# Weights of a mixture of experts loaded two chunks at a time, in 1 MB transfers of 8 KB per partition

## The chip, the cores and the metric

The kernel runs on one core of one Trainium2 chip. The metric is the device time of one execution in microseconds (us); lower is better.

## The reference

One layer over 2048 tokens of 1024 channels in fp32: a mixer (a long convolution over half of the channels, a Fourier transform over the other half, head norms and an output projection), then a mixture of 32 experts of which each token takes two, then a last norm. What matters here is the experts' part:

```python
def expert_block(args):
    e, rows_tok, rows_w = args
    xb = tok[rows_tok]                      # 128 tokens x 1024
    a = xb @ w_gate[e]                      # 1024 x 512
    u = xb @ w_up[e]                        # 1024 x 512
    y = (jax.nn.silu(a) * u) @ w_down[e]    # 512 x 1024
    return (y * rows_w[:, None].astype(y.dtype)).astype(tok.dtype)
...
out = jnp.zeros((T, D), tok.dtype).at[row_tok].add(ys.reshape(n_rows, D))
```

The three weight matrices of an expert have 2 MB each, 192 MB in all.

## The kernel before

The mixer fills the first half of the time. Routing then sorts the 32 experts by their counts into turns; `eid` holds the expert of each turn, and `gia`, `gib`, `sia`, `sib` hold the rows to gather and to add to. Each expert has 128 slots. The experts of the first 18 ranks (`RANK[e] < NOV`) have 32 more slots, the overflow tokens, whose rows are gathered as four quarters on four groups of 32 partitions (`xo`).

**Chunks.** `seq` lists 384 chunks of weights of 512 KB: four for each of gate, up and down of each expert, in the order of use. `load(n)` (L862) allocates a raw tile of 128 x 1024 fp32 and starts its transfer, on SP's queue for nearly all chunks and on POOL's for the eight of the first experts' down matrices. A gate or up chunk is 256 rows of 512 columns, row block k on columns 512 k of the tile (L880); a down chunk is 128 rows of 1024 columns (L883). The raw tiles rotate through three rings: 16 buffers (`NRAW`, tag `wr`), 4 (`NEXT`) and 4 (`NMORE`). The first 16 chunks are loaded while the mixer's last tiles are at work (L1357), the others by `take` (L1401), which hands out the next chunk for use and calls `load` up to 28 chunks ahead. A load waits on its queue until its buffer is free.

**Cuts.** `cut(n)` (L1387) splits a raw chunk into two parts in fp32r: ACT rounds it to `h` (L1391) and DVE takes the rest `l` (L1392; POOL for every second chunk of the last 24). Cuts run two chunks ahead of their use.

**Products.** `turn(e)` (L1525) transposes the 128 gathered rows `xg` with eight products against the identity on PE (L1533) and splits them into `xh` and `xl`; `turn_o(e)` (L1539) transposes the overflow rows `xo` with two (L1546). `gate_up` (L1550) makes six products of 512 columns for each chunk (L1563). `over` (L1575) multiplies the overflow tokens with the raw chunks in fp32, each product on one of four groups of 32 columns of the array (L1583); it runs once for the four chunks of a matrix, so these buffers come free together. `turn_s` (L1600) transposes the inner activations `s` (L1607) and, for overflow tokens, `so` with two products over 64 partitions (L1615). `down` (L1619) multiplies with the down chunks (L1631, L1637), scales the result on ACT (`yt`) and adds it to the rows of `X2` in DRAM with accumulating scatters issued by POOL (L1650, L1652). `between` (L1654) puts `turn_s(e)` and `turn(e + 1)` into the middle of the product before, and gathers three experts ahead.

**The end.** `bulk` (L1429) reads the 16 tiles of `X2` back into the ring of `wr` buffers (L1437), squares them on ACT (L1427), scales them on DVE (L1453) and stores the output (L1454), while the last two experts are still at work; those get their norm in `finish` (L1475).

Instructions of one engine run in the order of the program as it was scheduled when built; a waiting instruction holds up those behind it on its engine or queue. The tiles' semaphores make a load wait for all readers of the buffer that it overwrites.

Of the kernel before, what the change touches and what calls it, by code (L numbers as in the profile page):

```python
# [9 lines left out]
F32 = mybir.dt.float32  # L10
# [9 lines left out]
P = 128  # L20
# [25 lines left out]
# experts are taken by their counts: the first ones get 32 slots beyond the 128  # L46
NFIX = 2
# the first experts' 128 slots take tokens of the first tiles only
# [13 lines left out]
def _ranks():  # L62
    """The rank by count of the expert at each turn."""
    n, few = NE - NFIX - NLAST, NE - NOV - NLAST
    many, rest = iter(range(NFIX, NOV)), iter(range(NOV, NE))
    mid = [next(rest) if (i + 1) * few // n > i * few // n else next(many) for i in range(n)]
    return list(range(NFIX)) + mid + list(rest)
# [18 lines left out]
def fft_tables(T):  # L86
    """A transform of 4096 points in two stages: n = 64 a + p, p = 16 m + g, k = r + 64 k2.

    The first one sums over a and turns by exp(-2 pi i r n / 4096), r = 0..31 (r = 0 stands for 0 and 32, both
    real before the turn); the second one sums over p.  # L90
    """
# [11 lines left out]
    w = first(64 * a[None, :, None] + 16 * m[None, None, :] + g[:, None, None])     # [g, a, m, comp]  # L103
    wu = np.zeros((16, 2, 2, 32, 2, 2, 2, 64))      # [g, m % 2, part of z, a, m // 2, pass, m % 2, comp]
# [9 lines left out]
    w = first(32 * np.arange(P)[None, :] + np.arange(32)[:, None]).reshape(32, 64, 2, 64)     # [q, a, x, comp]  # L114
# [25 lines left out]
    # the inverse leaves p in the order 4 g + m  # L140
# [5 lines left out]
def tables():  # L146
# [16 lines left out]
    # real and imaginary parts of a 64-point transform, two groups at once  # L163
# [6 lines left out]
    # transform over t, folded twice: t < 512, bins k = 2 k' + parity  # L170
# [14 lines left out]
    # routing: tokens, counted from one, in the order of their tiles; rows of ranks  # L185
# [6 lines left out]
    # order of the experts: their numbers as tie breakers, ranks of the turns, masks  # L192
# [14 lines left out]
def build(tc, I, out, dbg=None, upto=99):  # L207
# [4 lines left out]
    with es:  # L212
# [8 lines left out]
        # Fourier columns of tiles 0..3 and 8..11; those of tiles 15 - k and 7 - k, with the row that follows, are read backwards  # L221
# [16 lines left out]
        def rsq(dst, src, scale, pool, n, tag, ln=False):  # L238
            """dst = (src * scale + EPS) ** -0.5"""
# [9 lines left out]
            # one Newton step for what the tables leave  # L249
# [8 lines left out]
        # ------------------------------------------------------------------ mixer, first part  # L258
# [15 lines left out]
        with ExitStack() as e1, ExitStack() as e2:  # L274
# [31 lines left out]
            def cutg(hi, lo, w):  # L306
                """hi and lo of w times the first norm's gain, a number for every row."""
# [19 lines left out]
            def conv(c, wvec, sink):  # L327
                """Projection chunk c through the short filter, a quarter of t for every call; sink(q, piece)."""
# [33 lines left out]
            def to_rows(src, dst):  # L362
                """[channel, 512 t] to [t, channel] rows of DRAM, in one or two parts, after the next products."""
# [16 lines left out]
            def sinks(c):  # L380
                """Filter and use of chunk c: v (8..11) is kept for x1 (4..7), whose product with it is z."""
# [13 lines left out]
            with tc.tile_pool(name="pa", bufs=1) as pa:  # L395
                # per-channel vectors: short filter (3 x 12), its bias (12), gains of heads and of the first norm
# [57 lines left out]
            def wprime(g):  # L454
                """Fourier columns of the projection, with the transform along a head folded in."""
# [28 lines left out]
            def ktaps(q):  # L484
                """The filter's taps 32 i + q, and the absolute sum so far."""
# [30 lines left out]
            def ksum(kt):  # L516
                """The kernel's absolute sum; the skip weight goes in as a tap at lag 0."""
# [32 lines left out]
            # implicit filters' features: partitions = (half of t, feature)  # L550
# [46 lines left out]
            def spread():  # L597
                """Features of t on the lower half of the partitions, of 2048 - t on the upper one."""
# [44 lines left out]
            def fweights(h):  # L643
                """Weights of half h of the Fourier columns, in two parts."""
# [8 lines left out]
            def fourier(h, i, wh, wl, pm, dst=None):  # L653
                """Fourier columns of tile i, rows = t, to DRAM or to where they are used."""
# [68 lines left out]
            def prod(o, w, xh, xl):  # L723
                """o = w x, both in two parts."""
                for n, (a, b) in enumerate(((0, xh), (0, xl), (1, xh))):
                    T.matmul(o, w(a), b, start=n == 0, stop=n == 2)

            def residue(n):
# [6 lines left out]
                if n == 0:  # L735
                    # the real bins 0 and 32 and those between them
# [8 lines left out]
                else:  # L745
                    # real parts on the lower half of the partitions, imaginary ones on the upper half
# [35 lines left out]
            def begin(t):  # L782
                """Rows t and 1024 + t of the fold, the first half of the columns where the second one comes straight."""
# [9 lines left out]
            def pair(t):  # L793
                """Sums and differences of rows t and L - t, and of 1024 + t and 1024 - t."""
                rr = rrs.pop(t)
                pq = []
                for k in range(2):
                    # groups of 66 real parts and 62 imaginary ones
# [9 lines left out]
            # Fourier columns, rows = t  # L808
# [41 lines left out]
        # ------------------------------------------------------------------ Fourier mixing, output projection  # L850
# [11 lines left out]
        def load(n):  # L862
            e, m, c = seq[n]
            k = n % (NRAW + NEXT + NMORE)
            if k < NRAW:
                w = mw.tile([P, 1024], F32, tag="wr", bufs=NRAW, name="w")
            elif k < NRAW + NEXT:
                w = ring[0].tile([P, 1024], F32, tag="wx", bufs=NEXT, name="w")
            else:
                w = ring[1].tile([P, 1024], F32, tag="wx", bufs=NMORE, name="w")  # L870
# [8 lines left out]
            if m < 2:  # L879
                q.dma_start(w.rearrange("p (k f) -> p k f", k=2),  # L880
                            src[:, 256 * c:256 * c + 256, :].rearrange("a (k p) f -> p (a k) f", p=P))
            else:
                q.dma_start(w, src[:, P * c:P * c + P, :].rearrange("a p f -> p (a f)"))  # L883
            raws[n] = w
# [3 lines left out]
        def gather(e, part=(0, 1)):  # L888
# [4 lines left out]
            if 1 in part and RANK[e] < NOV:  # L893
                xo_[e] = mw.tile([P, 256], F32, tag="xo", bufs=2, name="xo")
                x = G.indirect_dma_start(xo_[e], None, XR.rearrange("t (q c) -> (t q) c", q=4),
                                     bass.IndirectOffsetOnAxis(ap=gb[:, e:e + 1], axis=0))
                if e < NFIX:
                    # the queue goes on with these cuts while the rows are unknown
# [3 lines left out]
        # the first gathers come before the last tiles' rows  # L902
# [5 lines left out]
        with ExitStack() as e3:  # L908
# [21 lines left out]
            def headnorm(pool, y, n=P, ln=False):  # L930
                """y [n, 8, 64] in place: every head over its root mean square."""
# [10 lines left out]
            def split_T(pool, y, rev=False):  # L942
                """[t, 512] to hi and lo of its transpose, [128 c, 4, 128 t]."""
# [11 lines left out]
            def mix(yh, yl, wh, wl, h):  # L955
                """Half h of the output columns."""
# [10 lines left out]
            def rows(t, o):  # L967
                """Tokens 16 i + o of t, even i on the lower half of the partitions and odd ones on the upper half."""
                return [(slice(64 * v, 64 * v + 64), t.rearrange("(j v g) d -> g v j d", g=NT, v=2)[o, v]) for v in range(2)]

            def d1(o):
                """Inverse of the long convolution's first stage, gate and head norm for tokens 16 i + o."""
# [17 lines left out]
            with tc.tile_pool(name="fo", bufs=1, side="right", reuse_waits="tile") as fo:  # L990
# [9 lines left out]
                # t = 512, which is its own partner  # L1000
# [14 lines left out]
                def fold(t, par):  # L1015
                    """Parity par of the bins wants the sum and the difference, the other one the difference and the sum."""
# [805 lines left out]
```

## Time and profile before

| | us |
|---|---|
| median of three runs | 1753.75 |
| lowest and highest | 1752.33, 1755.37 |
| span of the profiled execution | 1749.5 |
| PE busy in the span | 1622.4 (93%) |
| DVE busy | 1228.6 (70%) |
| ACT busy | 1040.4 (59%) |
| POOL busy | 477.4 (27%) |

The span runs from the first to the last instruction of one execution. The profiled execution's own time beside its span is not recorded; the median of the other runs is 4.25 us above it. Busy shares are averages over stages with different limits: the experts' stage begins near 970 us and ends near 1735 us. PE is TensorE's products, PEld its weight loads, DVE VectorE, ACT ScalarE, POOL GpSimd, SP the engine that issues most transfers; a name with q (SPq, PEldq) is that engine's sequencer. The tables of the profile name a product as output<-moving operand,stationary operand for products with two matrices; a transpose is shown with the identity first.

### The profile page before, as it was taken

What the parts mean: (1) busy time and instruction counts of PE and PEld (TensorE: products, weight loads), DVE (VectorE), ACT (ScalarE), POOL (GpSimd) and SP (SyncE); (2) the same over time, 40 slices, a digit from 0 to 9 for tenths busy, and PEclk for the clock granted to TensorE, in tenths of its full rate; (3) what the DMA queues carried; (4) which work ended last, traced back from release to release, by engine and by line L of the source; (5) the groups of instructions that cost most, each with busy time, mean ns of one, the idle gap of its engine ahead of it and who ended that gap; (6) DMA issues with size and microseconds to landing.
All of it is one profiled execution on the core that took longest, in us unless ns stands there. A gap on an engine that the chain in (4) does not pass through costs nothing.

```text
span 1749.5 us, 27286 instructions
## 1 busy us (share of the span) xinstructions
PE 1622.4 (93%) x9043; PEld 1225.8 (70%) x9043; DVE 1228.6 (70%) x2105; ACT 1040.4 (59%) x1694; POOL 477.4 (27%) x512
## 2 busy tenths in 40 slices
PE   7999999999998969999998899999999999999863
PEld 5766666778777848867766667777777777677642
DVE  7576554422899665556888878887888888788666
ACT  8444555545898552215444567776777777667772
POOL 0203444232332232005434222222222222222252
PEclk9999999999999969999998899999999999999986
DMA  7245676899665585478777599999999999999974
GB/s 253 85 124 175 196 220 199 217 281 254 197 202 171 188 278 201 167 199 266 219 257 252 210 372 336 338 339 330 347 336 337 304 355 337 307 334 340 311 285 179
DMA packets 234620, 450.30 MB, mean 257 GB/s; under 512 B 27020, under 2 KB 82277, under 8 KB 233325
## 3 DMA queue, kind: packets, MB, share of 16 engines
q1 hardware_dynamic: 164244, 324.64, 53.6%
q0 software_dynamic: 36384, 97.94, 20.6%
q10 hardware_dynamic: 33848, 25.95, 4.7%
q8 instruction: 73, 1.20, 0.3%
q14 instruction: 71, 0.57, 0.1%
HBM read 346.32 MB, written 103.43 MB: 257 GB/s over the span
## 4 chain that ended last, share of the span: by engine, by line
PE 58%; DMA 9%; DVE 8%; issue 7%; ACT 3%; POOL 2%; SPq 1%; ACTq 0%; POOLq 0%; DVEq 0%
PE pa L1563 17%; PE psd L961 8%; PE py L1631 8%; PE psm L323 6%; PE po L1583 3%; DMA X<-yt,sia 3%; PE po L1637 2%; PE pm L659 2%; PE psEO L1348 2%; PE pstr L1533 1%; PE psEO L983 1%; PE psk L488 1%; DMA YZ<-yz 1%; PE psm L659 1%; POOL acc L496 1%
## 5 line engine op out<-in xcount | busy, mean ns | idle before, releaser
L1392 DVE TENSOR_TENSOR l<-w,h 128x1024 fp32r<-128x1024 f32 x370 | 452.8, 1228 | 144.5 <-ACT h L1391 121.5
L1391 ACT CAST h<-w 128x1024 fp32r<-128x1024 f32 x384 | 402.8, 1050 | 182.0 <-PE pa L1563 130.2
L323 PE MATMUL psm<-hhi,wt 128*128 128x512 f32 x768 | 251.9, 399 | 0.2 <-ACT hhi L425 0.2
L1563 PE MATMUL pa<-l,xh 128*128 128x512 f32 x512 | 207.3, 405 | 22.0 <-DVE l L1392 13.4
L1563 PE MATMUL pa<-h,xh 128*128 128x512 f32 x512 | 209.6, 410 | 1.9 <-ACT xh L1534 1.7
L1563 PE MATMUL pa<-h,xl 128*128 128x512 f32 x512 | 207.1, 405 | 0.0
L323 PEld LDWEIGHTS psm<-hhi,wt 128*128 128x128 f32 x768 | 145.3, 190 | 41.9 <-issue 9.9
L323 PE MATMUL psm<-hlo,wt 128*128 128x512 f32 x384 | 152.7, 398 | 0.1
L1563 PEld LDWEIGHTS pa<-l,xh 128*128 128x128 f32 x512 | 99.2, 194 | 45.4 <-DVE l L1392 15.0
L1563 PEld LDWEIGHTS pa<-h,xh 128*128 128x128 f32 x512 | 99.1, 194 | 40.3 <-ACT xh L1534 6.7
L1563 PEld LDWEIGHTS pa<-h,xl 128*128 128x128 f32 x512 | 99.2, 194 | 25.1 <-issue 3.3
L892 POOL DMA_INDIRECT xg<-XR,gia x30 | 49.7, 1657 | 224.2 <-PE pstr L1533 180.6
L1631 PE MATMUL py<-h,sh 128*128 128x512 f32 x256 | 108.6, 424 | 2.3 <-ACT sh L1608 2.3
L1631 PE MATMUL py<-l,sh 128*128 128x512 f32 x256 | 104.8, 409 | 0.0
L1631 PE MATMUL py<-h,sl 128*128 128x512 f32 x256 | 102.4, 401 | 0.0
L323 PEld LDWEIGHTS psm<-hlo,wt 128*128 128x128 f32 x384 | 73.0, 190 | 20.4 <-issue 5.3
L1650 POOL DMA_INDIRECT X<-yt,sia x30 | 48.2, 1606 | 136.6 <-ACT yt L1646 133.6
L1652 POOL DMA_INDIRECT X<-yo,sib x18 | 38.0, 2111 | 145.7 <-issue 79.0
L720 POOL TENSOR_TENSOR yl<-yl,yh 128x512 fp32r<-128x512 f32 x32 | 46.7, 1464 | 108.0 <-ACT yh L719 83.4
L347 ACT COPY u<-psm 128x512 f32<-128x512 f32 x48 | 28.1, 585 | 78.6 <-PE psm L323 78.6
L1583 PE MATMUL po<-w,xot 128*32 128x256 f32 x1152 | 69.0, 382 | 0.0
L496 POOL TENSOR_TENSOR acc<-ab,acc 128x512 f32<-128x512 f32 x32 | 48.3, 1509 | 68.4 <-ACT ab L495 67.2
(464 smaller groups left out, 3669.3 us busy)
## 6 DMA issues: line engine op xcount, KB each, us to landing
w<-in_w_gate SPq DMA_DIRECT2D x128, 512.0 KB
w<-in_w_up SPq DMA_DIRECT2D x128, 512.0 KB
w<-in_w_down SPq DMA_DIRECT2D x120, 512.0 KB
xt<-in_x SPq DMA_DIRECT2D x31, 512.0 KB
de<-in_c_decay SPq DMA_DIRECT2D x32, 256.0 KB
YK<-yk ACTq DMA_DIRECT2D x32, 256.0 KB
z<-zT POOLq DMA_DIRECT2D x32, 256.0 KB, 5.7
YZ<-yz SPq DMA_DIRECT2D x64, 128.0 KB
```

Of the source, the lines that this page charges most:

```text
L323: T.matmul(pm, wt[:, a, d, :], b[q][:, d, :], start=n == 0, stop=n == 23)
L496: G.tensor_tensor(KS["acc"], ab, KS["acc"], op=ALU.add)
L659: T.matmul(pm, a[q][:, d, P * o:P * o + P], b[:, d, :], start=n == 0, stop=n == 23)
L720: e.tensor_tensor(yl, y, yh, op=ALU.subtract)
L892: G.indirect_dma_start(xg_[e], None, XR, bass.IndirectOffsetOnAxis(ap=ga[:, e:e + 1], axis=0))
L961: T.matmul(pd, a[:, c, :], b[:, c, 512 * h:512 * h + 512], start=n == 0, stop=n == 11)
L1391: cuts.append(A.copy(h, raws[n]))
L1392: x = (G if n in POOL_CUTS + TAIL_CUTS else V).tensor_tensor(l, raws[n], h, op=ALU.subtract)
L1563: T.matmul(pa[m], x[:, d, :], y[:, f], start=d == 0 and q == 0, stop=d == 7 and q == 2)
L1583: T.matmul(po_[e][32 * j:32 * j + 32, 256 * m:256 * m + 256], xoT[e][:, k, b, :], w[:, 256 * j:256 * j + 256], start=b == 0, stop=b == 3, ...
L1631: T.matmul(py[i], x[:, c, :], y[:, f], start=c == 0 and q == 0, stop=c == 3 and q == 2)
L1650: G.indirect_dma_start(X2, bass.IndirectOffsetOnAxis(ap=sia[:, e:e + 1], axis=0), yt, None, compute_op=ALU.add)
```

## The change

`load` does nothing for odd chunks. For even ones it allocates a tile of 128 x 2048 fp32 (8 KB in each partition) from rings of half as many buffers and starts one transfer of 1 MB for chunks n and n + 1; each partition takes consecutive rows of the matrix, four of gate or up, two of down. A chunk is then one half of a tile. So contraction step k of a chunk pair holds rows 4 p + k (gate, up) or 2 p + k (down) in partition p, and the other operands follow: the transposes of `xg` take every fourth column, those of `s` and `so` every second one. The overflow rows are gathered as two halves of 2 KB on 64 partitions in place of four quarters of 1 KB on 128, and `turn_o` transposes them with four products over 64 partitions, every fourth column each. `bulk` reads two tiles of `X2` with one transfer. `lT`, a small tile of the routing, shares the buffer of `trf`. Comments are taken out.

```diff
         def load(n):
+            if n % 2:
+                return
             e, m, c = seq[n]
             k = n % (NRAW + NEXT + NMORE)
             if k < NRAW:
-                w = mw.tile([P, 1024], F32, tag="wr", bufs=NRAW, name="w")
+                w = mw.tile([P, 2048], F32, tag="wr", bufs=NRAW // 2, name="w")
             elif k < NRAW + NEXT:
-                w = ring[0].tile([P, 1024], F32, tag="wx", bufs=NEXT, name="w")
+                w = ring[0].tile([P, 2048], F32, tag="wx", bufs=NEXT // 2, name="w")
             else:
-                w = ring[1].tile([P, 1024], F32, tag="wx", bufs=NMORE, name="w")
+                w = ring[1].tile([P, 2048], F32, tag="wx", bufs=NMORE // 2, name="w")
...
-            if m < 2:
-                q.dma_start(w.rearrange("p (k f) -> p k f", k=2),
-                            src[:, 256 * c:256 * c + 256, :].rearrange("a (k p) f -> p (a k) f", p=P))
-            else:
-                q.dma_start(w, src[:, P * c:P * c + P, :].rearrange("a p f -> p (a f)"))
-            raws[n] = w
+            r = (256 if m < 2 else P) * c
+            u = 4 if m < 2 else 2
+            q.dma_start(w, src[:, r:r + P * u, :].rearrange("a (p k) f -> p (a k f)", k=u))
+            raws[n], raws[n + 1] = w[:, 0:1024], w[:, 1024:2048]
...
-                xo_[e] = mw.tile([P, 256], F32, tag="xo", bufs=2, name="xo")
-                x = G.indirect_dma_start(xo_[e], None, XR.rearrange("t (q c) -> (t q) c", q=4),
-                                     bass.IndirectOffsetOnAxis(ap=gb[:, e:e + 1], axis=0))
+                xo_[e] = mw.tile([64, 512], F32, tag="xo", bufs=2, name="xo")
+                x = G.indirect_dma_start(xo_[e], None, XR.rearrange("t (q c) -> (t q) c", q=2),
+                                     bass.IndirectOffsetOnAxis(ap=gb[0:64, e:e + 1], axis=0))
...
-                        V.tensor_scalar(dst, f, 4.0, cpt[:, 4:5], op0=ALU.mult, op1=ALU.add)
+                        V.tensor_scalar(dst[0:64], f[0:64], 2.0, cpt[0:64, 4:5], op0=ALU.mult, op1=ALU.add)
...
-                        lT = pd_.tile([P, P], F32, name="lT")
+                        lT = pd_.tile([P, P], F32, tag="trf", name="lT")
...
                 def read(o):
-                    xts[o] = mw.tile([P, D], F32, tag="wr", bufs=NRAW, name="xt")
-                    S.dma_start(xts[o], X2[P * o:P * o + P, :])
+                    if o % 2 == 0:
+                        xt = mw.tile([P, 2, D], F32, tag="wr", bufs=NRAW // 2, name="xt")
+                        S.dma_start(xt, X2[P * o:P * o + 2 * P, :].rearrange("(a p) d -> p a d", p=P))
+                        xts[o], xts[o + 1] = xt[:, 0, :], xt[:, 1, :]
...
                     for d in range(4):
-                        T.transpose(pt[:, d, :], xg[:, P * (4 * h + d):P * (4 * h + d) + P], ident)
+                        T.transpose(pt[:, d, :], xg[:, 512 * h + d:512 * h + 512:4], ident)
...
-                xot = mp.tile([P, 2, 4, 32], F32, tag="xot", bufs=2, name="xot")
+                xot = mp.tile([P, 4, 2, 32], F32, tag="xot", bufs=2, name="xot")
                 pt = pstr()
-                for k in range(2):
-                    T.transpose(pt[:, P * k:P * k + P], xo[:, P * k:P * k + P], ident)
+                for k in range(4):
+                    T.transpose(pt[:, 64 * k:64 * k + 64], xo[:, k:512:4], ident[:64, :64])
...
-                            T.matmul(po_[e][32 * j:32 * j + 32, 256 * m:256 * m + 256], xoT[e][:, k, b, :],
+                            T.matmul(po_[e][32 * j:32 * j + 32, 256 * m:256 * m + 256], xoT[e][:, 2 * (b % 2) + k, b // 2, :],
...
                 for j in range(4):
-                    T.transpose(pt[:, j, :], s[:, P * j:P * j + P], ident)
+                    T.transpose(pt[:, j, :], s[:, 256 * (j // 2) + j % 2:256 * (j // 2) + 256:2], ident)
...
                 for i in range(2):
-                    T.transpose(pt[:, 64 * i:64 * i + 64], so_[e][:, P * i:P * i + P], ident[:64, :64])
+                    T.transpose(pt[:, 64 * i:64 * i + 64], so_[e][:, i:256:2], ident[:64, :64])
```

## Rows read from the trace of the kernel before

**Rows 1.** The page: span and instructions.
```profile
span 1749.5 us, 27286 instructions
```

**Rows 2.** Windows: PE, PEld, DVE, ACT, POOL busy, clock, DMA, GB/s; then L1391 alone.
```profile
1010.00:1640.00 630.00, 627.79 (x3959) 453.98 (x3960) 502.00 (x527) 449.54 (x533) 143.51 (x87) 1.00 0.99 337
...
1600.00:1700.00 100.00, 83.82 (x421) 61.75 (x420) 68.53 (x75) 70.36 (x95) 38.50 (x18) 0.90 0.86 289
...
1010.00:1640.00 630.00, 351.07 (x335) 1.00 0.99 337
```

**Rows 3.** Waits, 1010 to 1640: us in total, times, longest; SPq, ACT, DVE, PE.
```profile
SPq L880 <- PE po L1583: 152.8, 56, 11.0
SPq L883 <- PE po L1637: 110.8, 31, 5.1
...
ACT h L1391 <- DMA w<-in_w_up: 3.0, 4, 1.3
...
DVE l L1392 <- DMA w<-in_w_gate: 6.7, 3, 2.2
...
PE pa L1563 <- ACT xh L1534: 1.7, 3, 0.6
```

**Rows 4.** DMA issues: queue, count, size, median us to landing where known.
```profile
cs<-in_c_ldft POOLq DMA_DIRECT2D x8, 1024.0 KB, 7.2
...
w<-in_w_down POOLq DMA_DIRECT2D x8, 512.0 KB, 8.5
```

**Rows 5.** PE's timeline around L1546 and L1615: start, us, instructions.
```profile
1238.36 0.48 PE L1631 MATMUL py<-h,sl 128*128 128x512 f32 x1
1238.67 0.38 PE L1546 MATMUL pstr<-ident,xo 128*128 128x128 f32 x2
...
1239.13 0.40 PE L1631 MATMUL py<-l,sh 128*128 128x512 f32 x1
1239.36 0.39 PE L1631 MATMUL py<-h,sl 128*128 128x512 f32 x1
...
1260.59 0.39 PE L1631 MATMUL py<-h,sh 128*128 128x512 f32 x1
1260.93 0.34 PE L1615 MATMUL pstr<-ident,so 64*128 64x64 f32 x2
...
1261.54 0.39 PE L1631 MATMUL py<-h,sl 128*128 128x512 f32 x1
```

**Rows 6.** Waits of PE's weight loads, 1010 to 1640.
```profile
PEld pstr L1615 <- issue: 4.0, 12, 0.4
```

**Rows 7.** Groups by form, PEld and PE: busy us, mean ns, idle before.
```profile
L1533 PEld LDWEIGHTS pstr<-ident,xg 128*128 128x128 f32 x256 | 30.5, 143 | 5.0 <-DVE sl L1609 1.0 <-PE psEO L1348 0.5
...
L488 PEld LDWEIGHTS psk<-wf,feat 128*64 128x64 f32 x128 | 11.9, 207 | 12.6 <-issue 6.8 <-ACT yk L513 5.4 <-DVE kt L493 0.4
...
L983 PEld LDWEIGHTS psEO<-zd,wi 128*64 128x64 f32 x64 | 3.8, 137 | 3.8 <-issue 3.1 <-DVE hv L242 0.4
...
L1615 PEld LDWEIGHTS pstr<-ident,so 64*128 64x128 f32 x36 | 3.6, 137 | 5.9 <-issue 4.3 <-DVE so L1597 1.5
...
L1533 PE MATMUL pstr<-ident,xg 128*128 128x128 f32 x256 | 36.4, 278 | 0.4 <-DMA xg<-XR,gfix 0.4
...
L1615 PE MATMUL pstr<-ident,so 64*128 64x64 f32 x36 | 5.8, 242 | 0.3
```

**Rows 8.** The tail: the chain in time order, then PE's and ACT's timelines.
```profile
1645.89 10.23 DMA X<-yt,sia
...
1661.86 5.90 DMA X<-yt,sia
...
1661.34 0.79 PE L1563 MATMUL pa<-l,xh 128*128 128x512 f32 x1 [5.97 <-POOL l L1392]
...
1671.50 1.06 ACT L1427 ACTIVATE jk<-xt 128x1024 f32<-128x1024 f32 x1 [2.00 <-DMA xt<-X]
...
1673.49 1.05 ACT L1427 ACTIVATE jk<-xt 128x1024 f32<-128x1024 f32 x1
```

## The prediction

> **What bounds the kernel now.** The page comes first: the span is 1749.5 us [rows 1]. The median of the three runs shown is 1753.75 us, 4.25 us more; the profile has no figure for what lies around its span, so I carry these 4.25 us as a constant and make the sum against the span. About 0.2% of the time, 3.5 us, is what a measurement of this kernel can tell from no change.
>
> Next the stages. The weights belong to the experts' stage, so its rows decide. From 1010 to 1640 us PE is busy for 627.79 of 630 us, and the DMA engines show 0.99 at 337 GB/s [rows 2]. Both look full, and the reader has to find out which of the two waits for the other. The waits tell it. The weights' queue waits for buffers to come free: 152.8 us for the products of the overflow tokens (po, L1583) and 110.8 us for those at L1637 [rows 3]. In the other direction the cuts wait for weights in single rows of 3.0 us and 6.7 us, and the only wait that reaches PE is 1.7 us for xh [rows 3]. So transfers wait for PE and PE does not wait for transfers. A full DMA share here is a queue that always has work, not a limit.
>
> The cover can be put in numbers. 335 casts in 630 us make one chunk of weights every 1.88 us [rows 2]. There are 24 chunk buffers (16 + 4 + 4), so a load is issued up to 24 x 1.88 = 45 us before its use; even with four chunks lost to the products that read a whole matrix at once, 37 us are left. A half-megabyte load of this kind lands in 8.5 us where the profile times it [rows 4].
>
> **The loads.** 384 transfers of 512 KB become 192 of 1 MB. The trace has one 1 MB transfer of the new shape, 8 KB per partition: it lands in 7.2 us [rows 4]. A pair is released when its second chunk is released, 1.88 us later for half of the chunks, and its first half is usable only when both have landed. I bound that by one whole landing, so the cover falls from 37 us less 8.5 us by at most 1.88 + 7.2 us and stays near 19 us: price 0. If the cover were gone, each late pair would stall the casts, and PE two chunks later. Half as many issues on SP and four fewer on POOL also cost or give nothing, as nothing on the path waits for them.
>
> **What follows the new row order, on PE.** PE has no idle time in this stage, so each added nanosecond there goes to the end. Four pieces change.
>
> First, turn_o (L1546). Today the overflow rows are turned by two transposes over 128 partitions; after the change by four over 64 partitions. The price of an inserted group is read from the starts of the full products around it. Around the pair of L1546, 1238.36 to 1239.13, with one more full product between, is 0.77 us for two ordinary steps of 0.23 us (1239.13 to 1239.36), so the pair costs 0.31 us [rows 5]. The narrow shape stands in the trace too: so (L1615) is turned by two transposes over 64 partitions. Around it, 1260.59 to 1261.54 is 0.95 us, again two ordinary steps, so this pair costs 0.49 us although each of its products has half the columns [rows 5]. The reason shows in the weight loads: 12 times in this stage the load for L1615 sat idle 0.33 us on average (4.0 us in all) with no engine to wait for [rows 6]. A change of the array's shape is paid, and the overflow rows join it. Each further narrow transpose adds 0.10 us (the two span 0.34 us, one lasts 0.242 us on average [rows 5, 7]). So four cost 0.49 + 2 x 0.10 = 0.69 us against 0.31: +0.38 us. 18 experts have overflow (NOV): +6.8 us. Bounds: if further ones are free, 18 x 0.18 = +3.2 us; if each of the two has its whole load of 0.137 us in the open and all four loads carry the stride's surcharge below (0.07 us), 1.04 - 0.31 = 0.73 us, times 18 = +13.1 us.
>
> Second, the transposes of xg (L1533) now load every fourth column. The trace has no such load with a step of four, but it has one with a step of 32: feat at L488, 128 x 64, takes 207 ns, and wi at L983, the same shape with columns side by side, takes 137 ns [rows 7]. So the step costs at most 0.07 us a load, and at least nothing, as the load of the next transpose runs under the product of this one. 256 x 0.07 = +17.9 us and 0 are the ends. I take +1 us, near the lower one: with the surcharge a load is 143 + 70 = 213 ns, still shorter than the 278 ns of the product beside which it runs [rows 7], and the first load of each group runs beside a full product of 512 columns.
>
> Third, s (L1607, 128 loads) and so (L1615, 36) are read with a step of two. The same ends, 164 x 0.07 = +11.5 us and 0; I take 0, as a step of 8 bytes is far nearer to side by side than one of 128 bytes.
>
> The Trainium skill speaks to these two: SBUF — State Buffer, section "Door 1: The DMA port swizzle", says that the memory is read in lines of 16 bytes, that two hits in a line are needed for full rate, and that each access to a new line pays. A step of four fp32 words makes every access a new line and a step of two does not, so by this rule xg pays and s and so do not. The rows above agree for a step of 32, and no row shows a step of four; taken with the full surcharge the sum below would be higher by 17 us, which is a rival.
>
> Fourth, the gather of xo moves 64 rows of 2 KB in place of 128 of 1 KB, ordered three experts ahead; no row shows a wait for it: 0.
>
> **The tail.** Here DMA is on the path. The accumulating scatter X<-yt takes 10.23 us at 1645.9 while the last weights are still arriving, and 5.90 us at 1661.9 when they are not [rows 8]. POOL waits for it in order with a cut of weights behind, and PE stalls 5.97 us for that cut [rows 8]. From 1600 to 1700 us the mean granted clock of PE is 0.90 [rows 2]: of its two levels, 2.4 and 1.2 GHz, the lower one held for a fifth of the stretch, and 10 us of work at full clock are lost. The weights' pieces grow from 2 and 4 KB to 8 KB and share the engines with the scatter's 4 KB rows. Ends: the 4.3 us of contention gone and the lost 10 us of clock with them, or 4.3 us once more, -14.3 to +4.3 us; I take +1 us, since the amount of weights in flight does not change and only the piece between two rows of the scatter gets longer.
>
> The last norm reads X two tiles at a time. ACT waited 2.00 us for the first tile until 1671.50 and squared the second one without a wait at 1673.49 [rows 8], so a pair is there by then: 0 to +2.0 us; I take +1 us. Casts of weights stand behind that square on ACT, and PE behind them.
>
> **Sum.** +6.8 + 1 + 0 + 1 + 1 = +9.8 us: a span of 1759.3 us, with the constant 1763.6, say 1764 us. From the bounds: 3.2 - 14.3 = -11.1 us at the least, 13.1 + 17.9 + 11.5 + 4.3 + 2.0 = 48.8 us if everything went wrong together.
>
> **Rivals.**
> Strided loads set the pace: the surcharge is paid at each of the 256 loads of xg and 72 of xo. 18 + 5 us on top of 1764, less the 1 us counted: 1786 us. For it: L488. Against it: loads run under products in this stage. It decides from 0.04 us on by which L1533's transposes stand further apart (10 us, as much as the rest of the sum).
>
> No change: the four narrow transposes fall beside the overflow products or those of so, where the shape changes anyway. Then only 4 x 0.10 - 0.31 = 0.09 us is added 18 times, 1.6 us, and if the tail costs nothing the time is 1755 us. Against it: today the pair of L1546 mostly stands alone among full products, as in rows 5.
>
> Faster: larger transfers clear the last weights out of the scatter's way. If the scatter at 1645.9 took the 5.90 us of the later one, 4.3 us of PE's stall would go, and with a shorter stall up to 10 us of clock: 1753.75 + 6.8 - 14.3 = 1746 us with the narrow transposes paid. It decides once it gives back more than 6.8 + 3.5 = 10.3 us. Against it: the last weights are issued as buffers come free at the same point, and pairs are released no earlier. DMA: Bandwidth & Descriptors of the Trainium skill, section "Rules for kernel authors", advises 1 MiB or more per transfer for full bandwidth; the rows of landing times (7.2 us for 1 MB, 8.5 us for half of it) agree, but this gain has no taker while PE waits for no load.
>
> **Chances.** Forecast, slower by 5 to 15 us: 0.50. Strided loads at the full price: 0.14. No change: 0.19. Faster: 0.17. That gives slower 0.64, same 0.19, faster 0.17. The range runs from 1750 us, which takes in the no-change case and the edge of the faster one, to 1780 us, which takes in the forecast's upper bounds and a part of the strided case. The forecast alone: 1757 to 1770 us.
>
> **What would show it.** Right: four narrow transposes at turn_o with an idle weight load of about 0.3 us ahead of them and 0.6 to 0.8 us between the full products around them; PE as full as now from 1010 to 1640 us with the same work ending some 8 us later; no new wait of PE or of the casts for weights. Wrong: rows in which PE or the casts wait for weights (the cover was mis-read); transposes of xg or s further apart (strides); the pair's replacement at the old 0.31 us; or a tail that moves by more than 4 us in either direction, because POOL, ACT and DVE each work in order there and a different order of a few instructions could outweigh the rest.

## Result and profile after: 13 us slower, nearly all of it on PE between full products

The changed kernel takes 1766.13 us (median of four runs, 1764.2 to 1770.9) against 1753.04 us for the kernel before beside it: a ratio of 1.0082, 95% interval 1.0061 to 1.0102. 1764 us was predicted, with a range of 1750 to 1780. Runs of one kernel spread by some 10 us in the experiments below, so this section reads the two profiled executions, whose inner stretches repeat far better.

First the page and the windows of the changed kernel, the last row with the casts (now L1392) alone; they answer to [rows 1, 2].

```profile
span 1763.4 us, 26394 instructions
PE 1637.8 (93%) x9079; PEld 1240.7 (70%) x9079; DVE 1227.6 (70%) x2105; ACT 1041.3 (59%) x1694; POOL 478.8 (27%) x508
```

```profile
1010.00:1640.00 630.00, 628.48 (x3937) 458.46 (x3936) 490.67 (x515) 441.57 (x523) 137.22 (x86) 1.00 0.94 330
1600.00:1700.00 100.00, 87.79 (x465) 65.89 (x464) 66.30 (x65) 67.69 (x84) 29.97 (x16) 0.95 0.86 298
...
1010.00:1640.00 630.00, 341.43 (x325) 1.00 0.94 330
```

The span is 13.9 us longer. PE is as full as before and gets through less: 325 casts in the 630 us against 335. The DMA engines show 0.94 against 0.99. The size of the transfers is not what frees them: the run with 1 MB transfers and the old row order (e1, below) shows 0.99 at the same 337 GB/s as before. It goes with the pieces of 8 KB: the kernels below that have them show 0.93 to 0.97 (e6 0.95 at 337 GB/s), those with 2 and 4 KB 0.99 to 1.00. The waits from 1010 to 1640 us (us in total, times, longest) say who takes that up, and answer to [rows 3].

```profile
SPq L884 <- PE po L1586: 189.2, 63, 10.6
SPq L884 <- DVE l L1393: 186.9, 70, 5.0
SPq L884 <- PE po L1640: 154.2, 33, 6.5
...
ACT h L1392 <- DMA w<-in_w_up: 0.3, 1, 0.3
ACT h L1392 <- DMA w<-in_w_gate: 0.3, 1, 0.3
...
PE pa L1566 <- ACT xh L1537: 1.5, 3, 0.5
```

Nobody does. The waits of ACT and DVE for weights fall from 11.4 us (9.7 us of it in the two rows of [rows 3]) to 0.6 us, but PE waited for none of them; the queue waits longer for buffers.

Where the time goes is seen between two fixed points: the first transposes of xg of turn 2 and of turn 29 (start and duration in us; the kernel before, then the changed one).

```profile
1008.09 1.03 PE L1533 MATMUL pstr<-ident,xg 128*128 128x128 f32 x8
...
1623.38 1.04 PE L1533 MATMUL pstr<-ident,xg 128*128 128x128 f32 x8
...
1010.06 1.11 PE L1536 MATMUL pstr<-ident,xg 128*128 128x128 f32 x8
...
1638.32 1.12 PE L1536 MATMUL pstr<-ident,xg 128*128 128x128 f32 x8
```

From start to start this is 615.29 us before and 628.26 us after. I call this **the stretch**; it holds the full-rate part of the experts' stage, and 13.0 of the 13.9 us. Of the rest, 2.0 us lie ahead of it and 0.2 us in turns 30 and 31, and from the last turn's transposes to the end it is 99.73 us against 100.98, 1.25 us less. The delay grows in steps: from one turn to the next the transposes of xg come 0.05 to 0.15 us later than before where the expert has no overflow tokens, and 0.5 to 0.85 us later where it has.

PE's timeline shows the two narrow groups between full products (start, us), to be read beside [rows 5].

```profile
1244.92 0.48 PE L1634 MATMUL py<-h,sl 128*128 128x512 f32 x1
1245.34 0.69 PE L1549 MATMUL pstr<-ident,xo 64*128 64x64 f32 x4
1245.96 0.50 PE L1634 MATMUL py<-h,sh 128*128 128x512 f32 x1
1246.30 0.40 PE L1634 MATMUL py<-l,sh 128*128 128x512 f32 x1
...
1267.78 0.40 PE L1634 MATMUL py<-h,sh 128*128 128x512 f32 x1
1268.11 0.45 PE L1618 MATMUL pstr<-ident,so 64*128 64x64 f32 x2
1268.49 0.50 PE L1634 MATMUL py<-l,sh 128*128 128x512 f32 x1
1268.82 0.39 PE L1634 MATMUL py<-h,sl 128*128 128x512 f32 x1
```

By the prediction's method, 1244.92 to 1246.30 less two steps of 0.23 us is 0.92 us for the group of four (median of 14 such places: 0.90); 1267.78 to 1268.82 gives 0.58 us for the pair of so, 0.49 before. The weight loads (mean ns behind the busy time) have grown, which the prediction had priced near nothing; the last row is the idle time ahead of the group of xo from 1010 to 1640 us, of which the prediction expected about 0.3 us each time.

```profile
L1536 PEld LDWEIGHTS pstr<-ident,xg 128*128 128x128 f32 x256 | 37.0, 208 | 5.0 <-issue 2.2 <-DVE sl L1612 0.7
L1610 PEld LDWEIGHTS pstr<-ident,s 128*128 128x128 f32 x128 | 18.8, 206 | 13.1 <-issue 7.8 <-DVE s L1572 4.3
L1549 PEld LDWEIGHTS pstr<-ident,xo 64*128 64x128 f32 x72 | 9.9, 209 | 5.4 <-issue 3.3 <-DVE xl L1538 2.1
L1618 PEld LDWEIGHTS pstr<-ident,so 64*128 64x128 f32 x36 | 5.6, 203 | 5.2 <-issue 2.9 <-DVE so L1600 1.4
...
PEld pstr L1549 <- issue: 2.7, 11, 0.2
```

Every load with a step takes 203 to 209 ns on average, be the step two (s, so) or four (xg, xo); with columns side by side it was 137 (so) and 143 (xg) [rows 7].

### The profile page after: what moved, and what is told of

It reads as the page before. It is cut to its first block, busy times and chain, and to the rows that moved or that the text cites. A ratio compares the mean times of both kernels' runs of the same rounds, so it can differ in the third digit from the quotient of the medians.

```text
span 1763.4 us, 26394 instructions
## 1 busy us (share of the span) xinstructions
PE 1637.8 (93%) x9079; PEld 1240.7 (70%) x9079; DVE 1227.6 (70%) x2105; ACT 1041.3 (59%) x1694; POOL 478.8 (27%) x508
## 5 line engine op out<-in xcount | busy, mean ns | idle before, releaser
L1392 ACT CAST h<-w 128x1024 fp32r<-128x1024 f32 x384 | 402.5, 1050 | 193.8 <-PE pa L1566 139.1
L1653 POOL DMA_INDIRECT X<-yt,sia x30 | 52.2, 1740 | 153.0 <-ACT yt L1649 144.6
L1655 POOL DMA_INDIRECT X<-yo,sib x18 | 33.6, 1869 | 151.9 <-issue 68.1
```

What stands on the lines that cost most here:

```text
L1392: cuts.append(A.copy(h, raws[n]))
L1653: G.indirect_dma_start(X2, bass.IndirectOffsetOnAxis(ap=sia[:, e:e + 1], axis=0), yt, None, compute_op=ALU.add)
L1655: G.indirect_dma_start(X4, bass.IndirectOffsetOnAxis(ap=sib[:, e:e + 1], axis=0), yo, None, compute_op=ALU.add)
```

## Experiments

All groups are medians over the places where they stand alone between full products, read as above. "Tail" runs from the last turn's transposes of xg to the end of the profiled execution. The medians are of 12 runs where nothing else is said (after 4, e4 6, e5 10). Each ratio compares with runs of the kernel before on the same chip, whose medians are 1751.04 to 1753.04 us, and not with the first row.

| kernel | median us | ratio to before (95%) | stretch | tail |
|---|---|---|---|---|
| before | 1753.04 | | 615.29 | 100.98 |
| after | 1766.13 | 1.0082 (1.0061 to 1.0102) | 628.26 | 99.73 |
| e1 loads alone | 1752.41 | 1.0002 (0.9987 to 1.0018) | 615.31 | 101.25 |
| e2 turn_o alone | 1755.09 | 1.0026 (1.0012 to 1.0041) | 619.86 | 99.09 |
| e3 no steps | 1756.77 | 1.0021 (1.0008 to 1.0034) | 619.86 | 102.86 |
| e4 full rows | 1759.87 | 1.0042 (1.0025 to 1.0059) | 618.98 | 101.91 |
| e5 so over full rows | 1746.94 | 0.9972 (0.9953 to 0.9990) | 610.78 | 101.17 |
| e6 permuted rows | 1757.46 | 1.0034 (1.0020 to 1.0048) | 615.02 | 100.42 |
| e7 look-ahead 12 | 1773.63 (one run) | | 628.24 | 105.50 |
| e8 look-ahead 6 | 1790.75 (one run) | | 628.23 | 125.33 |
| e9 full rows, no steps | 1753.44 (one run) | | 614.36 | 101.98 |
| e10 e5 with 1 MB loads | 1748.10 | 0.9979 (0.9966 to 0.9993) | 610.79 | 99.49 |
| e11 e5 again | 1748.88 | 0.9984 (0.9968 to 1.0001) | 610.88 | 100.80 |
| e12 16 buffers | 1785.47 (one run) | | 628.60 | 114.40 |

### The transfers alone (e1)

```diff
...
-            src[:, r:r + P * u, :].rearrange("a (p k) f -> p (a k f)", k=u)
+            src[:, r:r + P * u, :].rearrange("a (k p) f -> p (a k) f", p=P)
```

(against the changed kernel's load; all transposes and gathers as before)

> The kernel before with nothing but the transfers of 1 MB (pairs of chunks, rings of half as many buffers, the last norm's reads in pairs); inside a transfer each partition keeps its rows 128 apart, so no transpose and no gather changes. My theory: PE waits for no load in the experts' stage, so the transfers are worth nothing there and the tail moves by at most 2 us; time within 3 us of before (ratio 0.999 to 1.002), no more waits of the casts for weights than the 3.0 and 6.7 us of before. Rival, the transfers themselves cost the loss (pairs released later, both halves waited for): 8 to 13 us slower, ratio above 1.004. Rival, larger transfers are a gain that the transposes hide: faster by 4 us or more, ratio below 0.998.

The ratio is 1.0002 and the stretch is 615.31 us against 615.29. The 1 MB transfers, the release in pairs and the last norm's reads in pairs are neither gain nor loss.

### The overflow rows alone (e2), and the change without steps (e3)

```diff
 e2, against before: xo [64, 512], gathered in halves
...
-    T.transpose(pt[:, P * k:P * k + P], xo[:, P * k:P * k + P], ident)
+    T.transpose(pt[:, 64 * k:64 * k + 64], xo[:, P * k:P * k + P], ident[:64, :64])
...
 e3, against after
-    xg[:, 512 * h + d:512 * h + 512:4], xo[:, k:512:4], s[:, ...:2], so_[e][:, i:256:2]
+    xg[:, P * (4 * h + d):...], xo[:, P * k:P * k + P], s[:, P * j:...], so_[e][:, P * i:...]
```

> The kernel before with the overflow rows alone changed: gathered as two halves of 2 KB on 64 partitions and turned by four transposes over 64 partitions, columns side by side; weights, xg, s and so as before. From the profile after, the group of four costs 0.90 us between full products against 0.31 us before and 0.69 us in my prediction. Theory A, the price beyond 0.69 us comes from the step of four between columns (the loads take 0.21 in place of 0.14 us): the group costs 0.65 to 0.72 us here and the time rises by 18 x 0.38 = 6 to 7 us, ratio 1.0035 to 1.004. Theory B, four narrow transposes cost 0.9 us with any columns: 18 x 0.59 = 10 to 11 us, ratio near 1.006. If the whole loss comes from elsewhere: ratio within 0.001 of 1.

> The changed kernel with all its transposes taken from columns side by side (xg, xo, s, so), everything else as it is; the products then pair other rows of the weights with other columns, so the output is not the reference's and only the time is read. From the profile after: with steps the loads of the transposes take 0.205 to 0.21 us in place of 0.14, and the groups cost 0.96 in place of 0.88 (xg), 0.48 in place of 0.44 (s), 0.58 to 0.63 in place of 0.49 to 0.55 us (so). Theory A, a step of two costs as much as a step of four, and the steps are a part of the loss: 32 x 0.08 + 32 x 0.04 + 18 x 0.08 + 18 x 0.21 = 9 us less than the changed kernel, so about 4 to 5 us above before, ratio 1.002 to 1.003. Theory B, the longer loads are hidden under products and the groups moved for other reasons: as the changed kernel, ratio 1.007 to 1.009.

The timeline of e2 at the group of four:

```profile
1239.48 0.47 PE L1631 MATMUL py<-h,sl 128*128 128x512 f32 x1
1239.89 0.46 PE L1546 MATMUL pstr<-ident,xo 64*128 64x64 f32 x4
1240.28 0.50 PE L1631 MATMUL py<-h,sh 128*128 128x512 f32 x1
1240.61 0.40 PE L1631 MATMUL py<-l,sh 128*128 128x512 f32 x1
```

1239.48 to 1240.61 is 1.13 us, less 0.46 us: 0.67 us, as predicted for narrow transposes (0.69). With the step the same four products span 0.69 us in place of 0.46. Both kernels have the same stretch, 619.86 us, though one has the new loads and the other the old ones. So the stretch divides cleanly: 4.57 us for narrow transposes and 8.40 us for steps. Theory A holds for the groups and for the steps (9 us were expected of these). e2's time, 1.0026, came out under its 1.0035 to 1.004, as not every one of the 18 experts pays: from turn to turn e2 is 0.33 to 0.40 us later than before at 11 of the 16 places in the stretch, 0.19 to 0.23 us at three, where the old pair cost 0.44 us, and 0.03 to 0.04 us at two, where the group stands among overflow products.

### Shape against step (e4, e9)

```diff
-    xo_[e] = mw.tile([64, 512], ...)
+    xo_[e] = xoz[xon[0] % 2]      # two lasting tiles [P, 512], rows 64 and up zeroed once
...
-    T.transpose(pt[:, 64 * k:64 * k + 64], xo[:, k:512:4], ident[:64, :64])
+    T.transpose(pt[:, P * k:P * k + P], xo[:, k:512:4], ident)
 (so likewise; e9 besides with all columns side by side)
```

In both kernels the overflow rows of the first two experts are overwritten by a later gather; the work is the same.

> The changed kernel with the overflow rows (xo) and their inner activations (so) kept in tiles of 128 partitions whose upper 64 rows are zero, so that their transposes run over 128 partitions like all other products; as many transposes as before, each with 128 columns in place of 64, and the steps stay. Theory A, the change of the array's shape from 128 to 64 rows is the price: the four for xo fall from 0.90 to about 0.48 us (as the four of s), the two for so from 0.6 to about 0.25 us, 18 x 0.77 = 14 us less than the changed kernel, so about as fast as before, ratio 0.999 to 1.001. Theory B, it is the number of transposes: they are as many and wider, so no gain or a small loss, ratio 1.007 to 1.010. Between the two, about 1.004, if only one of the two groups stands alone often enough to pay for its shape.

> The fourth corner of shape and step: the changed kernel with xo and so in tiles of 128 partitions (upper 64 rows zero) and all transposes from columns side by side. The contraction no longer matches the row order, and the overflow rows of the first two experts are overwritten by a later gather, so only the time is read. So far the group of four transposes of xo costs 0.90 us narrow with steps, 0.67 narrow without, 0.56 over 128 partitions with steps. If shape and step simply add: 0.90 - 0.34 - 0.23 = 0.33 us. If the step only costs where the product is shorter than its weight load (64 columns), and 0.01 us a load over 128 partitions: 0.52 us, and the stretch from turn 2 to turn 29 near 614 us.

The timeline of e4 at xo and at so, and its waits of weight loads:

```profile
1243.85 0.48 PE L1643 MATMUL py<-h,sl 128*128 128x512 f32 x1
1244.17 0.63 PE L1555 MATMUL pstr<-ident,xo 128*128 128x128 f32 x4
...
1244.87 0.39 PE L1643 MATMUL py<-l,sh 128*128 128x512 f32 x1
...
1266.40 0.40 PE L1643 MATMUL py<-h,sh 128*128 128x512 f32 x1
1266.80 0.47 PE L1627 MATMUL pstr<-ident,so 128*128 128x128 f32 x2
...
1267.35 0.40 PE L1643 MATMUL py<-h,sl 128*128 128x512 f32 x1
```

```profile
PEld pstr L1627 <- issue: 4.9, 12, 0.4
PEld pstr L1555 <- DVE xl L1544: 2.2, 5, 0.4
```

| group of four for xo | narrow, 64 rows | 128 rows |
|---|---|---|
| step of four | 0.90 us | 0.56 us |
| side by side | 0.67 us | 0.52 us |

The four prices do not add: a step costs 0.23 us on narrow products and 0.04 us on wide ones, as the second theory of e9 said (its stretch is 614.36). For xo the idle load ahead is gone with the shape (no "issue" row for L1555, where the changed kernel has 11 places). For so it is not: 4.9 us in 12 places, with one shape throughout. The pair costs 0.49 us there, and of my theory A only the half on xo held, so the time came out between the two (1.0042). Of the time only a part is this: the stretch of e4 is 3.7 us longer than before, and another 4.0 us lie ahead of it, where before and e1 alone differ by 3.5 us.

### so over full rows in the kernel before (e5, e11), with large loads (e10)

```diff
-                so = mp.tile([64, 256], F32, tag="so", bufs=1, name="so")
+                so = soz[0][0:64]             # one lasting tile [P, 256], rows 64 and up zeroed once
...
-    T.transpose(pt[:, 64 * i:64 * i + 64], so_[e][:, P * i:P * i + P], ident[:64, :64])
+    T.transpose(pt[:, P * i:P * i + P], so_[e][:, P * i:P * i + P], ident)
```

> The kernel before with so kept in a tile of 128 partitions whose upper 64 rows are zero, so that its two transposes run over 128 partitions with 128 columns each; everything else as before. In the kernel before, this pair costs 0.49 to 0.55 us between full products, of which 0.33 us is an idle weight load ahead of it, put down by my prediction to the change of the array's shape. Theory A (the prediction's reading): with one shape the idle time goes and the pair costs about 0.31 us, as the pair of xo; 18 x 0.2 = 3 to 4 us less than before, and the stretch from the transposes of xg of turn 2 to those of turn 29 falls from 615.3 to about 612 us. Theory B (from the run with full rows, where the idle time ahead of so stayed, 4.9 us in 12 places): the idle time belongs to the place, the shape gives back only what the way out costs (0.15 against 0.03 us), so the pair costs 0.42 to 0.50 us, the stretch 613.5 to 615 us, and the time is within 2 us of before.

> The kernel before with so over 128 partitions (the pair of transposes that was 4.9 us faster by itself, ratio 0.9972) and with the 1 MB loads in the old row order (by themselves 1.0002). My theory: loads remain hidden when PE gets 4.5 us shorter, so the two just add: stretch 610.8 us to within 0.3, ratio 0.996 to 0.999, the same as so alone. Rival: with less work on PE the larger transfers show a gain or a loss: ratio below 0.995 or above 1.000.

> The kernel before with so over 128 partitions once more, beside the run with the larger loads on the same chip: ratio 0.996 to 0.999 and a stretch of 610.8 us if the first result holds, 1.000 if it was chance.

The timeline of e5 at so, and its idle loads:

```profile
1258.44 0.39 PE L1635 MATMUL py<-h,sh 128*128 128x512 f32 x1
1258.78 0.44 PE L1619 MATMUL pstr<-ident,so 128*128 128x128 f32 x2
...
1259.30 0.40 PE L1635 MATMUL py<-h,sl 128*128 128x512 f32 x1
```

```profile
PEld pstr L1619 <- issue: 3.1, 7, 0.4
PEld pstr L1619 <- DVE so L1601: 1.5, 4, 0.4
```

The pair alone falls from 0.49 to 0.55 us to 0.39 to 0.46, less than theory A said; the idle load stays in 7 of 12 places. Where the pair stands with s and overflow products (five places) 0.23 us go. Together 11 x 0.10 + 5 x 0.23 = 2.2 us, yet the stretch falls by 4.5 us, more than either theory. The rest comes together with another order of the build: where the 16 overflow products of a down matrix are split by transposes (seven places), they are so after 2 of them (2 and 14) in place of twice (6, 4 and 6). No run separates the two, so that the order is worth the other 2.3 us is argued and not shown. e4 and e9 have this order as well, so their stretches hold it beside the shape; their prices of single groups do not. In time e5 and e10 are faster than before, 0.9972 and 0.9979 with intervals below 1; e11, the same kernel as e5, has 0.9984 and reaches to 1.0001. The larger loads add nothing to it (610.79 against 610.78 us).

### The new row order met by the writers (e6)

```diff
 against after; xg, xo, s, so side by side, xo in quarters by two transposes over 128 partitions
-                        A.mul(xn, xf, rs)
+                            A.mul(prm(xn)[:, h], nat(xf)[:, h], rs)        # each h; positions (k, q) for channels 4 q + k
...
-                A.activation(s, pa[0], AF.Silu)
+                    A.activation(s[:, f].rearrange("p (j q) -> p q j", j=2), pa[0][:, f].rearrange("p (q j) -> p q j", j=2), AF.Silu)
```

> The changed kernel's loads (1 MB, 8 KB of consecutive rows in each partition), but the row order is met where XR, s and so are written, on ACT and DVE, whose outputs or inputs take the steps; xg, xo, s and so are then turned from columns side by side, xo as four quarters by two transposes over 128 partitions as in the kernel before. My theory: the loss is only steps and narrow transposes on PE, and ACT and DVE have room in this stage (80 and 71 of 100 us busy), so the stretch from turn 2 to turn 29 is back at 615.3 us (before) from 628.3, to within 0.5 us, and the time within 3 us of before (ratio 0.999 to 1.002). Rival: the steps on ACT and DVE make s late, PE waits for sh in the middle of each product, and the stretch is above 620 us. Rival: the 8 KB pieces cost something by themselves; the stretch stays above 616 us with no new wait for ACT or DVE.

The stretch is 615.02 us: 8 KB pieces cost nothing in it. But the time is 1.0034 of before, above the 0.999 to 1.002 that I expected. One place to look is the handoff from the mixer: from the start of the last transpose of the router (L1344 of before) to that of the first one of xg it is 4.2 us before and 5.8 us after, and in the changed kernel PE waits there for the first gather:

```profile
PE pstr L1536 <- DMA xg<-XR,gfix: 2.1, 1, 2.1
```

Before, PE waited 0.40 us for it [rows 7]. In six kernels with 8 KB pieces (after, e3, e4, e7, e8, e9) this handoff takes 5.0 to 5.8 us, in six with 2 and 4 KB pieces (before, e1, e2, e5, e10, e11) 3.5 to 4.7 us; e12, with 8 KB pieces and other loads there, has 2.0 us and does not fit. That larger pieces delay the first gathers is therefore argued and not shown. In e6 the handoff is 9.2 us, but there PE works on the router's products between the two and does not wait for the gather at all, so this figure shows another order of the build. Where the 4 us of e6 go stays open.

### How far the loads are covered (e7, e8, e12)

```diff
-LOAD_AHEAD = 28          e7: 12, e8: 6
-NEXT = 4, NMORE = 4      e12: 0, 0
```

> The changed kernel with loads issued at most 12 chunks ahead of use in place of 28 (LOAD_AHEAD), so 10 chunks or 18.8 us ahead of the cut. My prediction put the cover of the loads at 37 us less the landing of 8.5 us and less 9 us, about 19 us. Theory A, the cover is at least that: 18.8 us still hold a landing of 7 to 9 us, the stretch from turn 2 to turn 29 stays at 628.3 us to within 1 us. Theory B, transfers are near the limit of the DMA engines (0.94 of their time is shown busy) and need the depth: cuts and PE wait for weights and the stretch grows by more than 5 us.

> The changed kernel with loads issued at most 6 chunks ahead of use, so 4 chunks or 7.5 us ahead of the cut, about the landing time of 1 MB (7.2 us in the profile before). Here the cover is gone: the casts wait for weights at most pairs and PE after them; the stretch from turn 2 to turn 29 (628.3 us) grows by 20 us or more, some 0.1 to 0.5 us for each of 192 pairs at the least. Rival: transfers land in 4 to 5 us when few are under way, and even this costs less than 5 us.

> The changed kernel with 16 chunk buffers (8 pairs) in place of 24, the two small rings left out, so that loads are really issued later: the two runs with a smaller look-ahead issued the loads of the stretch at the same times as the changed kernel (1007.56 in place of 1007.52 us for the same load), because the buffers and not the look-ahead set their start, and so they tested nothing of the cover. Eight chunks less are 8 x 1.88 = 15 us less of cover. My theory, cover near 19 us: about 4 us are left, the stretch from turn 2 to turn 29 stays within 1 us of 628.3. Rival, the cover is smaller or the DMA engines need the depth: casts wait for weights by more than 20 us in all and the stretch grows by more than 5 us. The first experts, which hold 16 chunks at once, and the tail may be late in either case.

e7 and e8 did not test the cover: the look-ahead only orders the program, and the loads start when buffers come free, at the same times as in the changed kernel (1007.56 us in e8 and 1007.52 us there for the same load). They show something else. The queue of e8 in the tail:

```profile
SPq L1439 <- DMA X<-yt,sia: 47.0, 1, 47.0
```

The last loads now stand behind a read of X2 that waits 47 us for the scatters, and the tail grows by 26 us (in e7 the same wait is 36 us and the tail grows by 6). e12 does start loads later. From issue to the first cut of a pair it leaves 21.9 us (median; 18.0 at the least) in place of 37.8, and the stretch is 628.60 us, 0.34 more; ACT waits 5.2 us for weights in place of 0.6. The cover stands. The price is at the ends: 5 us more from turn 0 to turn 2 and 14.7 us in the tail.

## Why the prediction was right, point by point

**The bound and the loads at 0.** Right. Queue waits, e1, the equal stretches of e2 and e3, and e12 say the same. The 37 us from issue to use were read correctly (median 37.4 us from a load's issue to its cut in the trace of before, 37.8 in that of after). The landing was read from a spread: the eight transfers behind the 7.2 us took 5.1 to 12.3 us. With the longest, the same sum leaves 14 us, which changes nothing.

**turn_o, +6.8 us.** The right piece, with two errors that pull against each other. Narrow transposes alone cost 0.67 - 0.31 = 0.36 us as predicted, but only at 11 of the 16 places in the stretch; at three it is about 0.2 us, and at the two among overflow products nothing, as the "no change" rival had it for all. Together they are 4.57 us, where 16 x 0.38 = 6.1 us were predicted. The step, left out of the sum here, adds 0.23 us each, 3.7 us. Both make 8.3 us, inside the bounds (3.2 to 13.1), and with the step the group takes 0.90 us, outside the 0.6 to 0.8 us that were named as the sign. The mechanism behind the 0.49 us was half wrong. I put the idle load ahead of so down to the shape; in e4 it stays without a change of shape. What the shape does cost is seen at xo, 0.67 against 0.52 us for four.

**xg, +1 us.** Mis-sized. The groups of eight that stand alone cost 0.96 us against 0.88; 32 times 0.08 is 2.6 us. The surcharge per load is the 0.07 us that L488 showed, but PE's pace rises only from 0.109 to 0.120 us a transpose. The reason given for a value near nothing was a misreading: a load was compared with the 278 ns that a transpose lasts, while the transposes start 0.109 us apart. The rival "strided loads" at full price needed 0.04 us.

**s and so, 0.** The step that failed. "A step of 8 bytes is far nearer to side by side" was wrong: its loads take 206 and 203 ns, as with a step of four or 32. The groups rise from 0.44 to 0.48 us (s, 32 times: 1.2 us) and by 0.09 us (so, 18 times: 1.6 us). The rule of the Trainium skill that was cited for the zero (SBUF — State Buffer, "Door 1: The DMA port swizzle", two hits in a line for full rate) doesn't describe these weight loads: the step of two pays as much as the step of four.

**The tail, +2 us.** 1.25 us less in the one profile. The other kernels with their loads in the old places show tails of 99.1 to 102.9 us, so this term can't be told from nothing. The contention in it did grow, as its first +1 us took it. POOL's wait for the scatter that starts 2.7 us ahead of the last turn's transposes, and PE's waits for POOL's cuts in the tail, before and after:

```profile
POOL X L1652 <- DMA X<-yt,sia: 6.0, 1, 6.0
PE pa L1563 <- POOL l L1392: 8.6, 3, 6.0
...
POOL X L1655 <- DMA X<-yt,sia: 8.5, 1, 8.5
PE pa L1566 <- POOL l L1393: 12.6, 4, 7.9
```

From this scatter to the next one it is 12.3 to 13.5 us in six kernels with 8 KB pieces (after, e3, e4, e6, e9, e12) and 9.5 to 11.3 us in the six with 2 and 4 KB; e7 and e8, whose last loads come later, have 6.9 us. But PE's other waits shrink: in the tail it waits 32.1 us for all engines together, against 31.3, and the tail as a whole is not longer. The gain of the "faster" rival is not seen. The 2.0 us ahead of the stretch were not predicted and can't be told from nothing either: turn 2 starts at 1004.6 us in e1 and at 1007.9 us in e2, against 1008.1 before.

**The sum.** 9.8 us were predicted for the span and 13.9 measured, but not from the predicted parts, and that the two lie so near each other is in part luck. For the stretch the prediction has 6.1 us of narrow transposes and 0.8 us of steps; measured are 4.57 and 8.40 us (3.7 for xo, 1.7 for so, 3.0 for xg and s together). So two thirds of the loss in the stretch come from the steps, which it put near nothing. The narrow transposes, cheaper by 1.5 us, and a tail 3.3 us below its term hid part of that. The constant of 4.25 us hid some more: each timed run of the changed kernel lies 1.7 to 1.8 us above its own span, and with that the same sum says 1761 us.

## What to carry to other kernels

Transfers that nobody waits for were worth the same at 512 KB and at 1 MB; what their layout does to the operands of the engine that bounds the kernel was 13.0 of the 13.9 us. Small products between full ones are priced by the starts of their neighbours, and a strided weight load costs most where its product is short: here 0.23 us for four loads beside 64 columns, 0.04 us beside 128. One shape of the array, with zero rows where need be, is worth a try: e5, which has it for so and came out with another order besides, was 0.3% faster than the kernel before, and 0.2% in its repeat e11, whose interval just reaches no gain.

## What was not expected of the hardware

- A weight load takes 0.203 to 0.209 us with a step of two or four elements and 0.14 us without; in the groups of xo and xg it then paces transposes at 0.120 us each whether they have 64 columns (0.062 us side by side) or 128 (0.109 us).
- The weight load of the full product after a narrow group starts 0.15 us after the start of the group's last transpose, after a wide one 0.002 us; the product itself starts 0.152 and 0.028 us after it (e2 and e9, xo side by side).
- Zero rows cost less here than the change of shape: four 128 x 128 transposes with half of the rows empty take 0.52 us, four 64 x 64 ones 0.67 us.
- Pieces of 8 KB keep the DMA engines less busy for the same bytes (0.95 at 337 GB/s in e6, 0.99 at 337 GB/s before and in e1), and yet the scatter beside them took about 2 us longer.
